# Spacer tiles in SBUF that shift where the weights' halves, the activations and the heads' tiles begin (modulo 256 bytes)

## The chip, the cores and the metric

The kernel runs on one core of one Trainium2 chip. The metric is the device time of one execution in microseconds (us). Three runs of the kernel before took 2298.53, 2303.71 and 2309.76 us, a median of 2303.71 us.

## The reference

One layer of a streaming encoder on a sequence of 256 tokens of 2048 numbers, float32 throughout, conditioned on a vector `c`:

```
mod = silu(c) @ ada_w + ada_b                 # 9 shift/scale/gate vectors
x  += 1/2 * g1 * swiglu(modulate(rms(x)))     # 2048 -> 2 x 5632 -> 2048
h   = modulate(rms(x));  u = h @ w_in         # conv GLU, q, k, v, swish gate, two gates
y_conv = (silu(layer_norm(depthwise_conv31(a * sigmoid(b))))) @ conv_pw_w
y_ret  = (silu(g) * group_norm(retention(rotary(q), rotary(k), v))) @ ret_w_o   # 4 heads
x  += g2 * ((sigmoid(gate_c) * y_conv + sigmoid(gate_r) * y_ret) @ w_out)
x  += 1/2 * g3 * swiglu(modulate(rms(x)))
out = modulate(rms(x)) with its own shift and scale from c
```

Retention works in chunks of 64 tokens; the kernel computes it for a head as a masked 256 x 256 matrix of scores times the values.

## The kernel before, in words

Activations lie transposed: a tile has 128 features in the partitions and 256 tokens along the free dimension. Each weight matrix is read from memory once, in blocks of 128 rows by 128 columns that the host has laid side by side. `raw_load` (L100) brings up to 2048 columns (1 MB) into one of four `raw` buffers on SP's queue. `prep` (L178) then splits each half of it into two tiles of 1024 columns: `hi`, a copy by ScalarE to the type float32r (L189), and `lo`, the remainder `raw - hi`, by VectorE (L192). There are five buffers of each.

Activations are split in the same way, into halves that lie one behind the other: `h` (the modulated input, `new_h`, L259), `s2` (the hidden activations of a feed-forward block, called `s` in the profile, L337), `z` (the conv branch, L485), `r2` and `mg2` (the gated retention output and the merged branches, L595 and L631, called `r` and `mg` in the profile), `q_hi` and so on for the heads (L502).

Each product of two split numbers takes three matmuls: high times high, high times low, low times high. A matmul of TensorE (PE) has a stationary operand of 128 x 128, which a weight load (PEld) brings into the array ahead of it, and an operand that is streamed past it, here 256 columns. In the profile's names `ps<-h,hi` is a matmul that streams `h` past a block of `hi`. Every matmul has a weight load of its own. `gemm` (L206) does most of them: for the blocks of one `hi` tile, two matmuls each with `hi` (L216), then one each with `lo` (L218). `mm3` (L200) does the three in a row (L202, L203, L204). It is used where six PSUM banks are filled side by side from one block row (`across`, L320), in the heads, and in `value` (L523), where the roles are turned: there a slice of `h` is stationary and 512 columns of weights stream past it.

The stages in their order: the first feed-forward block (24 hidden tiles side by side, the rest by `gemm`; its second products stream `s`), the mixer's projections and four heads (`scores` streams q past k, `outputs` streams p past v), the gates and `w_o` (stream `h` and `r2` in turn), the conv branch's gate and `w_pw` (`h` and `z` in turn), `w_out` (streams `mg2`), the second feed-forward block, the final norm. In between, VectorE reduces the 176 tiles of the matrix for `mod` (L110) and applies the conv's taps (L443).

Tiles of a pool are laid out in SBUF in the order in which their tags are first asked for, and pools that are open at the same time lie one behind the other: `keep` (h, x and the constants), then `wp` (raw, a spacer of 64 bytes, hi, lo, a second spacer of 64 bytes), then the pool of the stage. A spacer is a tile that nothing reads; GpSimd (POOL) writes zeros to it once (`apart`, L92). The addresses come out of these sizes alone. A block of weights is 512 bytes of a partition, a half of an activation tile 1024, so all slices of a tile have the same remainder modulo 256. Before the change:

| tile | begins at, modulo 256 | as |
|---|---|---|
| h | 128 | streamed (stationary in `value`) |
| hi, lo | 192 | stationary (streamed in `value`) |
| s, z, r2, mg2 | 0 | streamed |
| q, p | 0 | streamed |
| k, v | 0 | stationary |

## Time and profile before

| | |
|---|---|
| median of three runs | 2303.71 us (2298.53 to 2309.76) |
| the profiled execution's own time | 2299.76 us |
| its span (first to last instruction) | 2298.0 us |
| PE, PEld busy | 98%, 97% |
| VectorE, ScalarE busy | 77%, 46% |
| granted TensorE clock | 0.995 |
| read from memory | 609.77 MB |

Busy time of PE is not PE at its peak: matmuls overlap in the array, a record covers more than the time that a matmul adds, and records in a row leave no gap. What a matmul adds is the distance from its start to the next one's. Where a stretch of the trace holds only matmuls of one kind and PE is never idle in it, that is the stretch's length by the number of matmuls. A stretch counts every record that touches it, so two that began ahead of it (a record of 0.28 us lasts over two distances) are taken off.

### The profile page before, as it was taken

The page shows a single profiled execution, that of the slowest core. Times are in us where ns is not written, and L with a number is a line of the kernel's source. Part 1 is how long each engine was busy: PE and PEld are TensorE (multiplying, and loading weights), DVE is VectorE, ACT ScalarE, POOL GpSimd, SP SyncE. Part 2 cuts the span into 40 slices and gives each one's busy share as a digit, 9 for nine tenths or more (in the row PEclk, how much of TensorE's full clock was granted, in tenths as well). Part 3 has the DMA queues.
Part 4 walks back from the last instruction along what each step waited for, and adds up shares of the span by engine and source line. Part 5 has one row for each costly group of instructions (what it writes and reads, how often), then busy time and mean ns, then how long its engine had stood idle before and what let it go on. Part 6 is the DMA issues. An engine that isn't in the chain of part 4 may idle for free.

```text
span 2298.0 us, 44555 instructions
## 1 busy us (share of the span) xinstructions
PE 2260.2 (98%) x19036; PEld 2234.0 (97%) x19036; DVE 1762.0 (77%) x2212; ACT 1068.4 (46%) x1367; POOL 0.4 (0%) x6
## 2 busy tenths in 40 slices
PE   7999999999999999999999999999999999999997
PEld 6999999999999999999999999999999999999997
DVE  7899887778877679889987787767766666666664
ACT  6544653334444644545544544445544433344443
POOL 0000000000000000000000000000000000000000
PEclk9999999999999999999999999999999999999999
DMA  9989689999888565545776788866777677777662
GB/s 342 357 326 334 222 303 338 328 332 344 335 316 306 173 216 200 170 165 203 266 248 242 261 329 303 332 250 243 288 262 273 243 254 259 269 265 271 248 247 74
DMA packets 92217, 616.86 MB, mean 268 GB/s; under 512 B 10225, under 2 KB 10481, under 8 KB 34673
## 3 DMA queue, kind: packets, MB, share of 16 engines
q1 hardware_dynamic: 90290, 609.81, 73.5%
q10 hardware_dynamic: 1728, 4.20, 0.5%
q8 instruction: 149, 2.44, 0.4%
q14 instruction: 50, 0.41, 0.0%
HBM read 609.77 MB, written 4.19 MB: 267 GB/s over the span
## 4 chain that ended last, share of the span: by engine, by line
PE 97%; DVE 1%; ACT 1%; issue 0%; DVEq 0%; ACTq 0%
PE ps L216 50%; PE ps L218 25%; PE ps L202 7%; PE ps L204 7%; PE ps L203 7%; DVE raw L110 0%; DVE f L668 0%; DVE ssq L272 0%; ACT L245 0%; ACT L238 0%; DVE lo L192 0%; PE gn_v L256 0%; PE gn_m L256 0%; ACT sq L288 0%; PE r L256 0%
## 5 line engine op out<-in xcount | busy, mean ns | idle before, releaser
L189 ACT CAST hi<-raw 128x1024 fp32r<-128x1024 f32 (+2 forms) x864 | 844.7, 986 | 1130.2 <-PE ps L216 639.2
L192 DVE TENSOR_TENSOR lo<-raw,hi 128x1024 fp32r<-128x1024 f32 (+2 forms) x864 | 980.1, 1143 | 452.0 <-ACT hi L189 430.7
L216 PE MATMUL ps<-h,hi 128*128 128x256 f32 x5888 | 731.1, 277 | 0.0
L216 PEld LDWEIGHTS ps<-h,hi 128*128 128x128 f32 x5888 | 698.1, 188 | 0.2
L110 DVE CUSTOM_DVE_ANT_0 raw<-raw,cb,vec 128x2048 f32<-128x2048 f32 x176 | 412.9, 2346 | 3.4 <-DMA raw<-in_adaT 3.4
L218 PE MATMUL ps<-h,lo 128*128 128x256 f32 x2944 | 395.2, 277 | 0.0
L216 PE MATMUL ps<-s,hi 128*128 128x256 f32 x2816 | 362.8, 279 | 0.0
L218 PEld LDWEIGHTS ps<-h,lo 128*128 128x128 f32 x2944 | 362.6, 188 | 0.0
L216 PEld LDWEIGHTS ps<-s,hi 128*128 128x128 f32 x2816 | 345.0, 188 | 0.0
L202 PE MATMUL ps<-h,hi 128*128 128x256 f32 x1152 | 313.8, 280 | 13.9 <-ACT h L305 13.8
L203 PE MATMUL ps<-h,hi 128*128 128x256 f32 x1152 | 318.8, 279 | 3.2 <-DVE h L308 3.2
L204 PE MATMUL ps<-h,lo 128*128 128x256 f32 x1152 | 315.9, 279 | 0.0
L202 PEld LDWEIGHTS ps<-h,hi 128*128 128x128 f32 x1152 | 216.5, 191 | 15.7 <-ACT h L305 15.3
L203 PEld LDWEIGHTS ps<-h,hi 128*128 128x128 f32 x1152 | 219.8, 191 | 3.9 <-DVE h L308 3.7
L204 PEld LDWEIGHTS ps<-h,lo 128*128 128x128 f32 x1152 | 218.1, 191 | 0.0
L218 PE MATMUL ps<-s,lo 128*128 128x256 f32 x1408 | 196.7, 279 | 0.0
L218 PEld LDWEIGHTS ps<-s,lo 128*128 128x128 f32 x1408 | 179.2, 188 | 0.0
L443 DVE SCALAR_TENSOR_TENSOR acc<-y,vec,acc 128x256 f32<-128x256 f32 x240 | 114.3, 481 | 2.7
L216 PE MATMUL ps<-r,hi 128*128 128x256 f32 x512 | 65.8, 280 | 0.0
L216 PE MATMUL ps<-mg,hi 128*128 128x256 f32 x512 | 65.7, 279 | 0.0
L216 PEld LDWEIGHTS ps<-r,hi 128*128 128x128 f32 x512 | 62.6, 188 | 0.0
L216 PEld LDWEIGHTS ps<-mg,hi 128*128 128x128 f32 x512 | 62.6, 188 | 0.0
(149 smaller groups left out, 1181.6 us busy)
## 6 DMA issues: line engine op xcount, KB each, us to landing
raw<-in_adaT SPq DMA_DIRECT2D x176, 1024.0 KB, 5.9
raw<-in_w SPq DMA_DIRECT2D x148, 1024.0 KB, 5.3
raw<-in_w SPq DMA_DIRECT2D x64, 896.0 KB, 5.6
raw<-in_w13s SPq DMA_DIRECT2D x64, 768.0 KB, 6.1
raw<-in_w_v SPq DMA_DIRECT2D x16, 1024.0 KB, 4.9
raw<-in_w_g SPq DMA_DIRECT2D x16, 1024.0 KB, 4.9
raw<-in_w_gr SPq DMA_DIRECT2D x16, 1024.0 KB, 4.9
raw<-in_w_o SPq DMA_DIRECT2D x16, 1024.0 KB, 5.3
```

The costliest lines, as they stand in the source:

```text
L110: tc.keep_in_program_order(V.tensor_tensor_reduce(r, r, cb, 1.0, vec[:, b:b + 1], op0=ALU.mult, op1=ALU.add, accum_out=mod[:, j, t:t + 1]))
L189: A.copy(hi[:, :c1 - c0], r[:, c0:c1])
L192: V.tensor_tensor(lo[:, :c1 - c0], r[:, c0:c1], hi[:, :c1 - c0].bitcast(F32), op=ALU.subtract)
L202: PE.matmul(o, st[0], mv[0], start=start, stop=False, skip_group_check=skip)
L203: PE.matmul(o, st[0], mv[1], start=False, stop=False, skip_group_check=skip)
L204: PE.matmul(o, st[1], mv[0], start=False, stop=stop, skip_group_check=skip)
L216: PE.matmul(o, w[k][0], mv[k][:, half], start=k == 0 and half == 0, stop=False)
L218: PE.matmul(o, w[k][1], mv[k][:, 0], start=False, stop=k == n - 1)
L443: tc.keep_in_program_order(V.scalar_tensor_tensor(out=acc[:, t], in0=y[:, t, k:k + T], scalar=vec[:, dw + k:dw + k + 1], in1=acc[:, t], op ...
```

## The change

It replaces the two spacers of 64 bytes by five of 128, 384, 128, 128 and 320 bytes, three of which lie in the pools of the mixer, and asks for `apart_k` between the tiles of q and k, so that `rotary` for q and for k are two statements:

```diff
-    def apart(i):
-
-        if i not in set_apart:
-            set_apart.add(i)
-            nc.gpsimd.memset(wp.tile([P, 16], F32, name=f"apart{i}", tag=f"apart{i}", bufs=1), 0.0)
+    def apart(pool, name, n):
+
+        if name not in set_apart:
+            set_apart.add(name)
+            nc.gpsimd.memset(pool.tile([P, n // 4], F32, name=name, tag=name, bufs=1), 0.0)
...
-            apart(0)
+            apart(wp, "apart_w", 128)
             hi = wp.tile([P, 1024], F32R, name="hi", tag="hi", bufs=HI)
             A.copy(hi[:, :c1 - c0], r[:, c0:c1])
             lo = wp.tile([P, 1024], F32R, name="lo", tag="lo", bufs=LO)
-            apart(1)
+            apart(wp, "apart_s", 384)
...
+                apart(p1, "apart_p", 128)
                 sc = t512("sc")
                 V.tensor_tensor(sc, two(ps), dm, op=ALU.mult)
                 return halves(sc, "p")
...
-            qk = [rotary(banks[0], "q"), rotary(banks[1], "k")]
+            qk = [rotary(banks[0], "q")]
+            apart(p1, "apart_k", 128)
+            qk.append(rotary(banks[1], "k"))
...
         with tc.tile_pool(name="mix2", bufs=1) as p2:
+            apart(p2, "apart_r", 320)
             r2 = sb(p2, [P, ND, 2, T], "r2", F32R)
```

What it does to the addresses, as the distance from the start of the stationary tile to the start of the streamed one, modulo 256:

| streamed past stationary | before | after |
|---|---|---|
| h past hi, lo | 192 | 128 |
| s past hi, lo | 64 | 128 |
| z past hi, lo | 64 | 128 |
| r2, mg2 past hi, lo | 64 | 192 |
| q past k; p past v | 0 | 128 |
| hi, lo past h (`value`) | 64 | 128 |

Modulo 512 the same distances are 192, 64, 64, 64, 0, 0 and 320 before, and 128 (h), 384 (s, z), 192 (r2, mg2), 384 (q), 128 (p) and 384 (`value`) after.

No instruction of PE, VectorE, ScalarE or SP is added, left out or moved. On GpSimd five memsets stand in the place of two; this is its program after the change, from the first spacer on, with what each waits for (a name in brackets is an engine's or a DMA queue's semaphore):

```order
L96 MEMSET apart_w 128x32
L96 MEMSET apart_s 128x96
L96 MEMSET apart_k 128x32 [waits DVE_49,PE_49]
L96 MEMSET apart_p 128x32
L96 MEMSET apart_r 128x80 [waits DMAHW4_49,DMAHW3_49,DMAHW5_49,DVE_49,DMAHW6_49,PE_49,Pool_49]
```

Four instructions of ScalarE and PE and one DMA of SP now wait for GpSimd too; all but one of them stand far behind the memset that they wait for. The one close by is a cast of ScalarE behind `apart_r`. These are ScalarE's rows after the change where the last head ends and the gates begin; `r_12204` is r2:

```order
L612 ACTIVATE g_12205<-ps 128x512 [waits PE_49]
L565 COPY og<-ps 128x512 [waits PE_49] x2
L189 CAST hi<-raw 128x1024 [waits DVE_49,PE_49]
L604 CAST r_12204<-g_12205 128x2x256 [waits DVE_49,Activation_49,Pool_49]
L189 CAST hi<-raw 128x1024 [waits DMAHW7_49,PE_49]
L457 ACTIVATE gn_mean<-gn_m 128x256 [waits PE_49]
```

The order of these rows is that of before; only the `Pool_49` of the first cast into r2 is new. Behind it in ScalarE's queue stand the casts of the next weights.

## The prediction

> **What bounds the kernel now.** I read the page's busy times and its chain first, then who waits for whom.

> ```profile
> PE 2260.2 (98%) x19036; PEld 2234.0 (97%) x19036; DVE 1762.0 (77%) x2212; ACT 1068.4 (46%) x1367; POOL 0.4 (0%) x6
> PE 97%; DVE 1%; ACT 1%; issue 0%; DVEq 0%; ACTq 0%
> ```

> ```profile
> ACT hi L189 <- PE ps L216: 639.2, 429, 4.4
> DVE lo L192 <- ACT hi L189: 430.7, 406, 3.7
> PE ps L202 <- ACT h L305: 13.8, 3, 5.8
> ```

> PE is the chain that ends last for 97% of the span. ScalarE, which makes the weights' halves, waits 639 us for PE to give a `hi` buffer back, and PE's own longest wait is 13.8 us, at the starts of stages. So the time is the number of matmuls times what each adds, and only a change of that number moves it. The groups of PE, by the tile that is streamed (first name) and loaded (second):

> ```profile
> line engine op names shapes xcount | busy us, mean ns | idle before us <-releasers
> L216 PE MATMUL ps<-h,hi 128*128 128x256 f32 x5888 | 731.1, 277 | 0.0
> L218 PE MATMUL ps<-h,lo 128*128 128x256 f32 x2944 | 395.2, 277 | 0.0
> L216 PE MATMUL ps<-s,hi 128*128 128x256 f32 x2816 | 362.8, 279 | 0.0
> L203 PE MATMUL ps<-h,hi 128*128 128x256 f32 x1152 | 318.8, 279 | 3.2 <-DVE h L308 3.2
> L204 PE MATMUL ps<-h,lo 128*128 128x256 f32 x1152 | 315.9, 279 | 0.0
> L202 PE MATMUL ps<-h,hi 128*128 128x256 f32 x1152 | 313.8, 280 | 13.9 <-ACT h L305 13.8
> L218 PE MATMUL ps<-s,lo 128*128 128x256 f32 x1408 | 196.7, 279 | 0.0
> L216 PE MATMUL ps<-r,hi 128*128 128x256 f32 x512 | 65.8, 280 | 0.0
> L216 PE MATMUL ps<-mg,hi 128*128 128x256 f32 x512 | 65.7, 279 | 0.0
> L202 PE MATMUL ps<-hi,h 128*128 128x512 f32 x128 | 50.6, 395 | 0.0
> L218 PE MATMUL ps<-mg,lo 128*128 128x256 f32 x256 | 35.4, 279 | 0.0
> L218 PE MATMUL ps<-r,lo 128*128 128x256 f32 x256 | 35.3, 279 | 0.0
> L216 PE MATMUL ps<-z,hi 128*128 128x256 f32 x256 | 32.8, 280 | 0.0
> L218 PE MATMUL ps<-z,lo 128*128 128x256 f32 x128 | 17.7, 279 | 0.0
> L203 PE MATMUL ps<-p_lo,v_hi 128*128 128x256 f32 x32 | 9.1, 283 | 0.0
> L204 PE MATMUL ps<-q_hi,k_lo 128*128 128x256 f32 x16 | 4.5, 283 | 0.0
> ```

> That is 12,288 matmuls with h, 4,224 with s, 384 with z, 1,536 with r and mg; p, q and `value` have three such groups each, 96, 48 and 384. All but `value` have the same shape. What each adds is read from stretches that hold one kind. The columns are the stretch, its length, then for each engine its busy time and instructions, the granted clock, the DMA's share and GB/s:

> ```profile
> 340.00:480.00 140.00, 140.00 (x1191) 140.00 (x1190) 111.68 (x130) 50.70 (x56) 0.00 (x0) 1.00 0.91 329
> 500.00:640.00 140.00, 140.00 (x1238) 140.00 (x1237) 111.45 (x118) 62.15 (x79) 0.00 (x0) 1.00 0.89 332
> 836.00:845.00 9.00, 9.00 (x41) 7.38 (x40) 9.00 (x18) 3.67 (x4) 0.00 (x0) 1.00 0.48 160
> 1048.00:1058.00 10.00, 10.00 (x90) 10.00 (x90) 9.77 (x15) 5.66 (x9) 0.00 (x0) 1.00 0.50 192
> 1059.00:1061.40 2.40, 2.40 (x22) 2.40 (x22) 2.40 (x5) 2.37 (x4) 0.00 (x0) 1.00 0.85 345
> 1068.00:1079.00 11.00, 11.00 (x96) 11.00 (x95) 9.59 (x12) 6.11 (x9) 0.00 (x0) 1.00 0.50 179
> 1345.00:1440.00 95.00, 95.00 (x809) 95.00 (x808) 75.33 (x77) 41.77 (x45) 0.00 (x0) 1.00 0.85 311
> 1455.00:1545.00 90.00, 90.00 (x767) 90.00 (x766) 66.02 (x74) 36.82 (x40) 0.00 (x0) 1.00 0.80 296
> ```

> PE is busy through each, at the full clock. With two records taken off for those begun earlier, s adds 140/1189 = 117.7 ns a matmul, h 140/1236 = 113.3, mg 90/765 = 117.6, p past v 2.4/20 = 120, and a 512-column matmul of `value` 9/39.3 = 229. Same engine, clock, shape and loop (s, h and mg all come from `gemm`), and neither VectorE nor DMA differs between the first two rows: what does is where the tiles lie. The distance from loaded to streamed is 192 for h, 64 for s, mg and `value`, and 0 for p. So a distance has a price here: 0 gives 120, 64 gives 117.7, 192 gives 113.3. But it is not all. The stretches 1068 to 1079 (11/94 = 117.0) and 1345 to 1440 (95/807 = 117.7) hold h at 192 too, alone and with z, and h there costs what s does. How many there are:

> ```profile
> L216 PE MATMUL ps<-h,hi 128*128 128x256 f32 x671 | 85.9, 281 | 0.0
> L218 PE MATMUL ps<-h,lo 128*128 128x256 f32 x336 | 46.4, 281 | 0.0
> ```

> ```profile
> L216 PE MATMUL ps<-h,hi 128*128 128x256 f32 x64 | 8.4, 284 | 0.0
> L218 PE MATMUL ps<-h,lo 128*128 128x256 f32 x31 | 4.3, 281 | 0.0
> ```

> The first pair is 1257.5 to 1452 us, the second 1068 to 1079: together 1,102 slow matmuls with h. Both stretches begin right behind the four plain float32 matmuls of a norm's sums; h has two regimes at one distance, and an interruption can move it from one to the other.

> **The change, part by part.** All prices but one are in the trace. r2 and mg2 go from 64 to 192: 1,536 times (117.7 - 113.3 = 4.4 ns) = 6.8 us less. Everything else goes to 128, which no matmul of before has. Its neighbours are 64 (117.7) and 192 (113.3), its opposite is 0 (120). From above I bound it by the nearer slow neighbour, 117.7. From below, a curve that is even around the circle (a mean plus a cosine) through the three prices has its mean at (117.7 + 113.3)/2 = 115.5 and gives 115.5 - (120 - 115.5) = 111.0 at 128. I take 113.3: the better neighbour, and the lowest value that any long stretch shows; h keeps to it in `gemm` and in `mm3` alike, which looks like a floor rather than a point on a curve, and the point farthest from the worst should be on it.

> By that value, s gives 4,224 x 4.4 = 18.6 us, z 384 x 4.4 = 1.7, the slow h 1,102 x 4.4 = 4.8, the other h nothing, p and q 144 x 6.7 = 1.0, and `value` 384 x (229 - 2 x 113.3 = 2.4) = 0.9. With r2 and mg2 the sum is 33.8 us.

> [...]

> What rides along is cheap. The memsets:

> ```profile
> L96 POOL MEMSET apart<- 128x16 f32 x2 | 0.2, 112 | 0.3 <-POOLq L756 0.3
> ```

> Three more at about 0.1 us, up to six times as wide, stay below 1 us each. Only the last has somebody near behind it, the first cast into r2, with casts of weights behind that. r2 itself is not streamed until all gates of that loop are done, and the `hi` casts have 639 us of waiting for PE to spend, five buffers ahead; if that cover were gone, the price would be one memset, under 1 us. VectorE's and ScalarE's operands move too; a few per cent on either would vanish in their 23% and 54% of idle time. Would a faster s stage starve? It would need 329 x 117.7/113.3 = 342 GB/s and a DMA share of 0.945; VectorE would be at 83%.

> ```profile
> GB/s 342 357 326 334 222 303 338 328 332 344 335 316 306 173 216 200 170 165 203 266 248 242 261 329 303 332 250 243 288 262 273 243 254 259 269 265 271 248 247 74
> ```

> The second slice moved 357, so it just fits. If it were held at 329, the first block's s (half of 18.6 us) would give nothing, 9.3 us back.

> **Rivals.** *Lower still.* At 128 the streams may clear each other entirely and 113.3 may itself hold a price. For it: three distances, three prices, and the curve through them leads to 111.0. Against: nothing in the trace stays below 113. All that goes to 128 is 12,288 + 4,224 + 384 + 144 = 17,040 matmuls; 2.3 ns less each is 39 us more, 73 us in all: 2227. [...]

> *Slower.* 128 may be like 64. Then h, which is two thirds of PE's time, leaves the best distance in the trace for the sake of tiles a third as many. The 11,186 fast matmuls with h would lose 4.4 ns each, 49.2 us; s, z and the slow h would gain nothing; r2 and mg2 would still give 6.8 and p and q 0.3: 42 us slower, 2342. Against the forecast it decides from a price of 113.3 + 33.8/17,040 us = 115.3 ns at 128. At 120, as for distance 0, it would be 80 us. For it: 113.3 is a regime that h can fall out of, and 192 may be special because of who comes first at a place, not because it is far. Against: 64 and 192 are equally far from 128, so a dependence by nearness favours the better half.

> *Nothing.* The price may hang on the regime that a run of matmuls enters, not on the distance (the 1,102 slow ones at 192 speak for it), or on addresses modulo 512, where s would be at 384 and h at 128, both unseen. If s, h, z stay as they are and only r2 and mg2 follow, 2293; if nothing follows, 2299.8. [...]

> **How the numbers follow.** The sum is made against the profiled execution's own 2299.8 us, of which 2298.0 are the span: 2299.8 - 33.8 = 2266. The median of the three runs is 3.9 us higher, and they lie 11 us apart; so 0.5%, 11.5 us, is about what a measurement of this kernel can tell from no change. Chances: the forecast, with slow stretches of h or DMA waits left over, 0.47; lower still 0.22; nothing or r2 and mg2 alone 0.12; slower 0.19. The range takes in the first three and their edges: from 2215, somewhat beyond 111.0 ns, to 2306, nothing at the median; most of the slower case stays outside. Faster by over 0.5%: 0.47 + 0.22 and a few mixed cases, 0.72. Within 0.5%: 0.10. Slower: 0.18.

> **What would show it.** The stretch of s (about 330 to 480 us) should hold a matmul every 113.3 ns, that is 1,238 records in 140 us rather than 1,191; h in 500 to 640 should stay at 1,238; mg should rise from 767 in 90 us to about 796; p past v should go from 0.12 us to 0.113. PE must stay busy through each, and ScalarE's wait for PE should shrink by some 30 us with no wait of PE for `hi` in its place. h with fewer than 1,215 records in 140 us (115.3 ns) proves the forecast wrong and the slower rival right; more than 1,250 proves the lower one. A shift in VectorE's or ScalarE's durations would not matter unless PE begins to wait.

## The result, and the profile after

The change makes the kernel slower: 2362.86 us (median of four runs, 2358.31 to 2367.42) against 2306.59 us (2298.53 to 2309.76), a ratio of 1.0249 with a 95% interval of 1.021 to 1.0289. Ratios that stand with an interval leave out any run over 1.5% above the fastest of its kernel. The forecast was 2266. Busy times and chain of the changed kernel:

```profile
PE 2318.5 (98%) x19036; PEld 2291.3 (97%) x19036; DVE 1765.6 (75%) x2212; ACT 1070.2 (45%) x1367; POOL 0.8 (0%) x9
PE 97%; DVE 1%; ACT 1%; issue 0%; DVEq 0%
```

PE bounds it as before, with the same number of matmuls. VectorE and ScalarE do the same work in the same time, 3.6 and 1.8 us more. PE's busy time grew by 58.3 us, the span by 58.5. So each matmul adds more. The stretches by stage (length, then busy time and count for PE, PEld, VectorE, ScalarE and GpSimd, then clock, DMA share and GB/s), in this order s, h, `value`, h behind a norm's sums, mg, h of the second block:

```profile
360.00:500.00 140.00, 140.00 (x1182) 140.00 (x1182) 112.59 (x131) 52.68 (x57) 0.00 (x0) 1.00 0.92 336
530.00:670.00 140.00, 140.00 (x1182) 140.00 (x1181) 107.53 (x112) 59.61 (x75) 0.00 (x0) 1.00 0.86 316
860.00:869.00 9.00, 9.00 (x40) 7.33 (x39) 9.00 (x19) 4.76 (x8) 0.00 (x0) 1.00 0.67 229
1115.00:1185.00 70.00, 70.00 (x586) 70.00 (x584) 65.66 (x91) 34.30 (x41) 0.00 (x0) 1.00 0.71 252
1500.00:1570.00 70.00, 70.00 (x620) 70.00 (x620) 54.63 (x60) 30.56 (x33) 0.00 (x0) 1.00 0.85 316
1600.00:1840.00 240.00, 240.00 (x2025) 240.00 (x2024) 160.66 (x197) 109.21 (x147) 0.00 (x0) 1.00 0.75 265
```

With two records taken off as before, h adds 140/1180 = 118.6 ns a matmul where it added 113.3. Its 1,182 records in 140 us are below the 1,215 named ahead as the sign of the slower rival. The s stretch has the same 118.6 (117.7 before). mg, the one tile here that went to 192, adds 70/618 = 113.3 (117.6 before). 128 has a second price as well: in the fourth stretch, h adds 70/584 = 119.9. That holds for 670 matmuls, behind the sums of a norm. h and s now have the same distance and the same price, although one is at 128 and the other at 384 modulo 512. h's own address did not change at all; only the weights that are loaded beside it moved.

The sum closes to about 1 us: 11,186 x 5.3 ns for h that was fast = 59.3 us, 1,102 x 0.9 for h that was slow = 1.0, 4,608 x 0.9 for s and z = 4.1, less 1,536 x 4.4 for r and mg = 6.8, makes 57.6. The 670 at the second price add 0.9. `value` rose too, from 229 to 9/38.3 = 235 in the stretches shown; over all its matmuls the distance from start to start rose from 229 to 232, which is 1.2 us for 384. That makes 59.7; measured were 58.5.

The new memsets on GpSimd cost nothing. The rows are the last of them, and ScalarE's longest wait:

```profile
L96 POOL MEMSET apart_r<- 128x80 f32 x1 | 0.2, 165 | 283.6 <-PE ps L204 283.6
ACT hi L189 <- PE ps L216: 684.9, 447, 2.1
```

`apart_r` takes 165 ns and starts at 1095.18 us. The first cast into r2, which waits for it, starts at 1097.95, right behind a cast of weights and with no idle time of ScalarE before it. ScalarE's wait for PE grew from 639 to 685 us: with a slower PE, ScalarE has more time to spare.

### The profile page after: what moved, and what is told of

Same layout as the page of the kernel before. It is cut to its first block, busy times and chain, and to the rows that moved or that the text cites. A ratio compares the mean times of both kernels' runs of the same rounds, so it can differ in the third digit from the quotient of the medians.

```text
span 2356.5 us, 44565 instructions
## 1 busy us (share of the span) xinstructions
PE 2318.5 (98%) x19036; PEld 2291.3 (97%) x19036; DVE 1765.6 (75%) x2212; ACT 1070.2 (45%) x1367; POOL 0.8 (0%) x9
## 4 chain that ended last, share of the span: by engine, by line
PE 97%; DVE 1%; ACT 1%; issue 0%; DVEq 0%
PE ps L216 50%; PE ps L218 25%; PE ps L202 7%; PE ps L203 7%; PE ps L204 7%; DVE f L672 0%; DVE raw L110 0%; DVE ssq L272 0%; ACT L245 0%; ACT L238 0%; DVE lo L192 0%; PE gn_v L256 0%; PE gn_m L256 0%; ACT sq L288 0%; PE r L256 0%
## 5 line engine op out<-in xcount | busy, mean ns | idle before, releaser
L189 ACT CAST hi<-raw 128x1024 fp32r<-128x1024 f32 (+2 forms) x864 | 846.2, 985 | 1189.1 <-PE ps L216 684.9
L192 DVE TENSOR_TENSOR lo<-raw,hi 128x1024 fp32r<-128x1024 f32 (+2 forms) x864 | 981.7, 1143 | 508.3 <-ACT hi L189 492.3
L216 PE MATMUL ps<-h,hi 128*128 128x256 f32 x5888 | 759.7, 282 | 0.0
L216 PEld LDWEIGHTS ps<-h,hi 128*128 128x128 f32 x5888 | 725.1, 188 | 0.2
L218 PE MATMUL ps<-h,lo 128*128 128x256 f32 x2944 | 409.7, 282 | 0.0
L218 PEld LDWEIGHTS ps<-h,lo 128*128 128x128 f32 x2944 | 375.2, 188 | 0.0
L216 PE MATMUL ps<-s,hi 128*128 128x256 f32 x2816 | 365.4, 281 | 0.0
L216 PEld LDWEIGHTS ps<-s,hi 128*128 128x128 f32 x2816 | 347.5, 188 | 0.0
L202 PE MATMUL ps<-h,hi 128*128 128x256 f32 x1152 | 319.4, 285 | 13.8 <-ACT h L305 13.8
L203 PE MATMUL ps<-h,hi 128*128 128x256 f32 x1152 | 324.7, 284 | 3.4 <-DVE h L308 3.4
L204 PE MATMUL ps<-h,lo 128*128 128x256 f32 x1152 | 321.7, 284 | 0.0
L202 PEld LDWEIGHTS ps<-h,hi 128*128 128x128 f32 x1152 | 216.7, 191 | 15.5 <-ACT h L305 15.3
L203 PEld LDWEIGHTS ps<-h,hi 128*128 128x128 f32 x1152 | 219.8, 191 | 4.1 <-DVE h L308 3.9
L204 PEld LDWEIGHTS ps<-h,lo 128*128 128x128 f32 x1152 | 218.3, 191 | 0.0
L218 PE MATMUL ps<-s,lo 128*128 128x256 f32 x1408 | 198.3, 281 | 0.0
L218 PEld LDWEIGHTS ps<-s,lo 128*128 128x128 f32 x1408 | 180.4, 188 | 0.0
L216 PE MATMUL ps<-r,hi 128*128 128x256 f32 x512 | 63.7, 277 | 0.0
L216 PE MATMUL ps<-mg,hi 128*128 128x256 f32 x512 | 63.4, 276 | 0.0
L216 PEld LDWEIGHTS ps<-r,hi 128*128 128x128 f32 x512 | 60.7, 188 | 0.0
L216 PEld LDWEIGHTS ps<-mg,hi 128*128 128x128 f32 x512 | 60.5, 188 | 0.0
```

The lines of the kernel that those rows point to most:

```text
L189: A.copy(hi[:, :c1 - c0], r[:, c0:c1])
L192: V.tensor_tensor(lo[:, :c1 - c0], r[:, c0:c1], hi[:, :c1 - c0].bitcast(F32), op=ALU.subtract)
L202: PE.matmul(o, st[0], mv[0], start=start, stop=False, skip_group_check=skip)
L203: PE.matmul(o, st[0], mv[1], start=False, stop=False, skip_group_check=skip)
L204: PE.matmul(o, st[1], mv[0], start=False, stop=stop, skip_group_check=skip)
L216: PE.matmul(o, w[k][0], mv[k][:, half], start=k == 0 and half == 0, stop=False)
```

## The experiments

Edits are against the changed kernel unless said otherwise; numbers in the code are bytes.

**h alone back to 192 (h_back).** A spacer ahead of `h`, and the next one shorter, so that the weights stay where the change put them:

```diff
+    nc.gpsimd.memset(keep.tile([P, 16], F32, name="apart_h", tag="apart_h", bufs=1), 0.0)
     crow = sb(keep, [1, D], "crow", tag="h")
...
-            apart(wp, "apart_w", 128)
+            apart(wp, "apart_w", 64)
```

> The changed kernel with h alone moved by 64 bytes (and what lies between h and the weights with it), so that h is 192 past hi and lo again, at another address than before; hi and lo stay where the change put them. Theory (distance): h falls from 118.7 to 113.4 ns, 12,288 x 5.3 = 65 us, to about 2298 to 2303 us, ratio to before 0.997 to 0.999; s stays at 118.7. Rival (where the weights' halves lie by themselves is what made h slow): h stays at 118.7, about 2363 us, ratio 1.025.

Measured: 2309.12 us (2305.85 to 2318.65, 10 runs), 1.0011 times the kernel before (0.9983 to 1.0039). Its stretches of h, s, and h again:

```profile
100.00:320.00 220.00, 220.00 (x1871) 220.00 (x1870) 194.41 (x272) 113.52 (x173) 0.00 (x0) 1.00 0.80 285
360.00:500.00 140.00, 140.00 (x1182) 140.00 (x1181) 112.22 (x131) 51.47 (x56) 0.00 (x0) 1.00 0.92 335
520.00:670.00 150.00, 150.00 (x1326) 150.00 (x1325) 119.34 (x127) 65.53 (x83) 0.00 (x0) 1.00 0.88 331
```

h is at 150/1324 = 113.3 again in 520 to 670, at an address that it never had, past weights that lie at 0 and not at 192; s stays at 118.6. So nearly all of the loss was h's distance of 128, and neither tile's place by itself. In this profile the first stretch of h, at the same 192, is in the slow regime (220/1869 = 117.7), and so is the one from 2020 to 2201 us (160/1359 = 117.7 from 2030 to 2190). That is why the time is some 7 us above the 2298 to 2303 expected.

**Everything at 192 (all192).**

```diff
-            apart(wp, "apart_w", 128)
+            apart(wp, "apart_w", 64)
...
-            apart(wp, "apart_s", 384)
+            apart(wp, "apart_s", 192)
...
-                apart(p1, "apart_p", 128)
+                apart(p1, "apart_p", 192)
...
-            apart(p1, "apart_k", 128)
+            apart(p1, "apart_k", 64)
...
-            apart(p2, "apart_r", 320)
```

> Every streamed tile 192 bytes past the weights it streams by (h, s, z, r2, mg2, q, p); value stays at 64. Theory (the distance from loaded to streamed, modulo 256, sets the price): 113.4 ns a matmul in the stretches of s, z, r and mg as for h, so some 33 us below the kernel before, ratio about 0.986; about 0.988 if h keeps its slow stretches. Rival (the price belongs to the tile or to the regime its stage falls into, and r2 and mg2 were lucky): s and z stay near 117.7, ratio 0.997 or above.

Measured: 2286.09 us, 0.9891 times the kernel before (0.9856 to 0.9925): faster than both kernels, by less than hoped, and the ten runs lie between 2267.57 and 2301.84. By the medians of all runs it is 2286.09/2302.93 = 0.993. Two stretches of h, one of s, then h again, s and h of the second block:

```profile
95.00:220.00 125.00, 125.00 (x1105) 125.00 (x1105) 115.32 (x147) 58.67 (x82) 0.00 (x0) 1.00 0.91 327
235.00:335.00 100.00, 100.00 (x851) 100.00 (x851) 84.16 (x129) 56.20 (x92) 0.00 (x0) 1.00 0.71 248
360.00:490.00 130.00, 130.00 (x1106) 130.00 (x1105) 101.90 (x121) 46.33 (x52) 0.00 (x0) 1.00 0.91 326
520.00:670.00 150.00, 150.00 (x1276) 150.00 (x1275) 116.73 (x122) 64.00 (x82) 0.00 (x0) 1.00 0.86 318
1880.00:2000.00 120.00, 120.00 (x1061) 120.00 (x1060) 79.16 (x90) 47.44 (x51) 0.00 (x0) 1.00 0.77 276
2030.00:2170.00 140.00, 140.00 (x1238) 140.00 (x1237) 91.12 (x96) 61.89 (x78) 0.00 (x0) 1.00 0.73 261
```

h starts at 125/1103 = 113.3, and in the second block s is at 120/1059 = 113.3 and h at 140/1236 = 113.3. From 227 until 845 us, though, h and s alike are at 117.7 to 117.8 (100/849, 130/1104, 150/1274). These are about 5,160 matmuls, each 4.4 ns dearer, 23 us in all; at the fast price, this execution of 2290.87 us would have taken 2268. So the distance sets which prices are to be had, 113.3 and 117.8 at 192, and the regime which of them is paid, whatever the tile. The moment of the change can be seen in the order of time (rows of PE, and the cast; rows of other engines between them are left out):

```profile
226.26 0.41 ACT L311 CAST h<-xr 128x256 fp32r<-128x256 f32 x1
226.28 0.28 PE L202 MATMUL ps<-h,hi 128*128 128x256 f32 x1
226.39 0.28 PE L203 MATMUL ps<-h,hi 128*128 128x256 f32 x1
226.50 0.28 PE L204 MATMUL ps<-h,lo 128*128 128x256 f32 x1
226.72 0.74 PE L202 MATMUL ps<-h,hi 128*128 128x256 f32 x4
```

Starts are 0.11 us apart until 226.50, and the next is 0.22 later: it starts 0.05 us behind the end of ScalarE's cast of the last piece of h, at 226.67. The four matmuls of the last row take 0.46 us from the first start to the last (0.74 less a record of 0.28), 0.11 more than three distances of 117.8 ns, so one of them is late too. From 235 us on the stretch above has them 117.8 ns apart.

**The same kernel again (all192_b)**, on the chip of the two kernels that follow it here.

> The kernel of all192 again, on the chip and in the rounds of the kick. Theory (two regimes, entered by chance): again a scatter of some 30 us, between 2267 (no slow stretch) and 2300; median 2275 to 2290. Rival (the scatter of all192 was that chip's): under 10 us of scatter.

Measured: 2288.83 us, six runs from 2269.32 to 2325.97, 0.9881 times the kernel before (0.983 to 0.9932), and 0.994 by the medians of all runs. The slowest run lies 26 us above the scatter that was expected. The profile is of an execution of 2271.13 us; its stretches of s, h and s again:

```profile
350.00:480.00 130.00, 130.00 (x1150) 130.00 (x1149) 102.81 (x121) 46.42 (x52) 0.00 (x0) 1.00 0.92 332
520.00:650.00 130.00, 130.00 (x1150) 130.00 (x1149) 107.08 (x112) 59.31 (x76) 0.00 (x0) 1.00 0.92 345
675.00:750.00 75.00, 75.00 (x639) 75.00 (x638) 56.30 (x62) 31.56 (x35) 0.00 (x0) 1.00 0.82 302
```

The s and h that were slow in the other profile are at 130/1148 = 113.2 here; only the third stretch is slow, at 75/637 = 117.7. That regime lasts from 668 to 753 us, 718 matmuls or 3 us more; at the fast price this execution, too, would have taken 2268 us. The forecast's price for s at 192 holds where the regime is fast, and DMA keeps up with it, at 332 GB/s in the stretch of s and 345 in that of h. The same program thus has stretches that are fast in one execution and slow in another, and the difference between the two profiled times is theirs.

**Other distances (sweep_a and sweep_b).** Two kernels with one distance to a tile, exchanged between them; this is the first:

```diff
-            apart(wp, "apart_w", 128)
+            apart(wp, "apart_w", 32)
...
-            apart(wp, "apart_s", 384)
+            apart(wp, "apart_s", 160)
...
+        apart(pool, "apart_z", 192)
         y = sb(pool, [P, NC, PAD + T + 2], "y")
...
-            apart(p2, "apart_r", 320)
+            apart(p2, "apart_r", 192)
```

Its `apart_p` and `apart_k` are 96. In the second kernel the four are 96, 224, 64 and 64, and the last two 224.

> Other distances, one to a tile: h 224, s 160, z 96, r2 and mg2 32, q 160, p 96. Theory (distance): one price per stretch, and the same for the same distance in the other sweep, whatever the tile; between known neighbours, about 117 for h (224), 116 for s (160), 118 for z (96), 119 for r and mg (32); about 2340 us. Rival (tile or regime): the same distance costs different tiles prices over 1 ns apart.

> The distances of the other sweep, exchanged: h 160, s 224, z 32, r2 and mg2 96, q 32, p 224. Theory (distance): h at what s had at 160, s at what h had at 224, z at what r had at 32, r and mg at what z had at 96, each within 0.5 ns; about 2330 us by neighbours. Rival (tile or regime): they keep the prices of their tiles.

Measured: 2355.83 and 2362.12 us, one execution each, 16 and 32 us above what was expected. The first kernel's stretches of h (224), s (160), s later (160) and mg (32):

```profile
100.00:320.00 220.00, 220.00 (x1862) 220.00 (x1861) 193.65 (x270) 111.99 (x171) 0.00 (x0) 1.00 0.80 282
360.00:500.00 140.00, 140.00 (x1196) 140.00 (x1195) 112.81 (x131) 51.28 (x57) 0.00 (x0) 1.00 0.94 338
700.00:770.00 70.00, 70.00 (x592) 70.00 (x592) 54.06 (x60) 29.63 (x32) 0.00 (x0) 1.00 0.85 312
1500.00:1570.00 70.00, 70.00 (x602) 70.00 (x601) 53.88 (x60) 29.72 (x32) 0.00 (x0) 1.00 0.82 307
```

And the second's, h (160), s (224), h later (160), mg (96), and z (32), for which only the matmuls with z are counted:

```profile
100.00:320.00 220.00, 220.00 (x1857) 220.00 (x1856) 193.44 (x269) 112.27 (x171) 0.00 (x0) 1.00 0.80 282
360.00:500.00 140.00, 140.00 (x1185) 140.00 (x1185) 110.50 (x129) 50.66 (x56) 0.00 (x0) 1.00 0.92 332
520.00:670.00 150.00, 150.00 (x1281) 150.00 (x1280) 117.51 (x124) 64.31 (x83) 0.00 (x0) 1.00 0.87 323
1500.00:1570.00 70.00, 70.00 (x586) 70.00 (x585) 53.54 (x59) 29.01 (x31) 0.00 (x0) 1.00 0.81 299
1385.00:1391.30 6.30, 5.82 (x48) 5.72 (x48) 0.00 (x0) 0.00 (x0) 1.00 0.72 241
```

224 costs h 220/1860 = 118.3 and s 140/1183 = 118.3. 160 has two regimes as well, and both tiles show both: s 117.3 and 70/590 = 118.6, h 118.6 and 150/1279 = 117.3. 32 costs mg 70/600 = 116.7, 96 costs it 70/584 = 119.9, and z at 96 in the first kernel costs 120.0. So the price follows the distance and not the tile, with one exception: z at 32 costs (5.82 - 0.28)/47 = 117.9 in each of its eight stretches, 1.2 ns more than mg, where at most 0.5 was expected. It may be a second price of 32. Or it counts that the two are 256 bytes apart modulo 512 (288 for z, 32 for mg). No run separates these. Of the values between, 160, 224 and 96 were guessed too low, and 32 too high.

**Half steps, and 512 (sweep_c).** The kernel with everything at 192, s 256 bytes further on, and h and r2 begun 16 bytes into longer tiles (mg2 in the same way):

```diff
-            apart(wp, "apart_s", 192)
+            apart(wp, "apart_s", 448)
...
-        return sb(keep, [P, ND, 2, T], "h", F32R)
+        full = sb(keep, [P, ND * 2 * T + 8], "h", F32R)
+        return full[:, 4:4 + ND * 2 * T].rearrange("p (n u t) -> p n u t", n=ND, u=2)
```

> Half steps beside 192: h at 176, r2 and mg2 at 208, by views that begin 16 bytes into their tiles; s and z at 192 modulo 256 but 448 modulo 512. Theory (distance modulo 256, with a notch at 192): s and z at 113.3 or 117.8; h and r between 113.3 and the prices of 160 and 224 (117.3 to 118.7). If the notch is as narrow as a line of 32 bytes, h and r are near 117 or above, about 2320 us; if 16 bytes don't matter, all is at 113.3, about 2270. Rival (512 counts): s and z above 118.

Measured: 2352.14 us, one execution. h (176), s (192), s of the second block, mg (208):

```profile
100.00:320.00 220.00, 220.00 (x1847) 220.00 (x1846) 192.27 (x268) 112.17 (x172) 0.00 (x0) 1.00 0.80 281
360.00:500.00 140.00, 140.00 (x1191) 140.00 (x1190) 108.57 (x129) 50.17 (x56) 0.00 (x0) 1.00 0.91 328
1920.00:2050.00 130.00, 130.00 (x1149) 130.00 (x1149) 87.45 (x97) 51.30 (x55) 0.00 (x0) 1.00 0.77 273
1500.00:1570.00 70.00, 70.00 (x590) 70.00 (x589) 53.38 (x60) 28.68 (x31) 0.00 (x0) 1.00 0.81 302
```

16 bytes to either side of 192 the gain is gone: h 220/1845 = 119.2, mg 70/588 = 119.0. s, at 192 modulo 256 but 448 modulo 512, has the two prices of 192, 117.7 and 130/1147 = 113.3. So at 192, as at 128 (h at 128 and s at 384 in the changed kernel, both at 118.6), 256 bytes more changed nothing, and 192 is a notch narrower than 16 bytes to a side. The time is 32 us above the 2320 expected because h was put at 117 and cost 119.2. Three more kernels (half_a, half_b and quarter) looked for others, with the weights' halves begun 16 or 8 bytes into wider tiles, four `lo` buffers instead of five, and spacers to suit:

```diff
-RAW, HI, LO = 4, 5, 5
+RAW, HI, LO = 4, 5, 4
...
-            hi = wp.tile([P, 1024], F32R, name="hi", tag="hi", bufs=HI)
+            hi = wp.tile([P, 1088], F32R, name="hi", tag="hi", bufs=HI)[:, 4:]
```

> The weights' halves begin 16 bytes into their tiles (four lo buffers instead of five make the room), so distances fall between the steps so far: h 16, s 48, z 80, r2 and mg2 112, q and p 64. Theory (192 is a notch and everything else lies at 116.5 to 120 ns): no stretch below 116, h and s about 118 to 119; about 2360 us. Rival (more notches lie between the steps): a stretch at 113.3 or below.

> As half_a with h 144, s 240, z 48, r2 and mg2 80. Theory (one notch): no stretch below 116 ns; z as s at 48 in half_a, r as z at 80 there, within 0.7 ns; about 2360 us. Rival (more notches): a stretch at 113.3 or below.

> As half_a with the halves 8 bytes into their tiles: h 184, s 248, z 56, r2 and mg2 120. Theory (the notch at 192 is narrower than 16 bytes): h at 184 tells whether 8 bytes are still within it; above 117 if it is a matter of 16-byte pieces, 113.3 if it is a slope. Everything else above 116; about 2360 us, or 2310 with h in the notch.

Measured: 2356.27, 2378.04 and 2354.46 us, one execution each. In the first, h (16), s (48), mg (112), h of the second block (16):

```profile
100.00:235.00 135.00, 135.00 (x1128) 135.00 (x1127) 118.88 (x149) 57.09 (x78) 0.00 (x0) 1.00 0.86 312
360.00:480.00 120.00, 120.00 (x1031) 120.00 (x1030) 93.50 (x110) 41.21 (x46) 0.00 (x0) 1.00 0.91 322
1500.00:1585.00 85.00, 85.00 (x710) 85.00 (x710) 62.21 (x71) 33.70 (x37) 0.00 (x0) 1.00 0.81 300
1600.00:1900.00 300.00, 300.00 (x2559) 300.00 (x2558) 203.20 (x248) 140.82 (x189) 0.00 (x0) 1.00 0.73 259
```

In the second, whose granted clock was 0.95 throughout, h (144), s (240), mg (80), and z (48) with its own matmuls alone:

```profile
100.00:250.00 150.00, 150.00 (x1252) 150.00 (x1251) 133.89 (x175) 70.11 (x101) 0.00 (x0) 0.95 0.86 307
360.00:500.00 140.00, 140.00 (x1186) 140.00 (x1185) 110.24 (x128) 49.21 (x56) 0.00 (x0) 0.95 0.91 327
1510.00:1580.00 70.00, 70.00 (x595) 70.00 (x594) 54.46 (x62) 29.28 (x32) 0.00 (x0) 0.95 0.86 322
1379.50:1386.00 6.50, 5.76 (x48) 5.68 (x48) 0.00 (x0) 0.00 (x0) 0.95 0.93 349
```

In the third, h (184) and s of the second block (248):

```profile
100.00:230.00 130.00, 130.00 (x1101) 130.00 (x1100) 115.85 (x147) 55.23 (x77) 0.00 (x0) 1.00 0.87 314
1925.00:2060.00 135.00, 135.00 (x1170) 135.00 (x1169) 87.93 (x97) 52.65 (x56) 0.00 (x0) 1.00 0.77 268
```

16 costs 135/1126 = 119.9 in the first block and 300/2557 = 117.3 in the second, so it has two prices too. 48 costs 120/1029 = 116.6, 112 85/708 = 120.1, 144 120.0, 240 118.2, 80 118.0, 184 130/1099 = 118.3, 248 135/1168 = 115.6; mg at 120, in the third kernel, 118.0 (595 records in 70 us). So the prices run from 115.6 to 120.1 without a slope that leads anywhere, but for one notch at 192, 8 bytes below which the price is already 118.3. Across tiles the prices agree here: z at 48 costs (5.76 - 0.28)/47 = 116.6 in the second kernel, as s does in the first. The theory's "no stretch below 116" missed 248 by 0.4 ns; nothing but 192 comes to 113.3.

**What changes the regime (kick and jolt).** The kernel with everything at 192, with two overwritten matmuls at distance 0 put in at 24 places (in `pair`, ahead of `across` in the first block as below, and at the start of `side_by_side`):

```diff
+    pairs_done = [0]
+    def kick(o, w):
+        for _ in range(2):
+            PE.matmul(o, w[0][2][:, 0:P], w[0][2][:, 0:T], start=True, stop=True)
...
-            gemm(ps[:, u * T:(u + 1) * T], ws[u](), mv)
+            w = ws[u]()
+            if u == 0 and pairs_done[0] % 12 == 0:
+                kick(ps[:, 0:T], w)
+            pairs_done[0] += u
+            gemm(ps[:, u * T:(u + 1) * T], w, mv)
...
+            if begins and i % 2 == 0:
+                kick(banks[0][:, 0:T], w)
```

> All at 192 as in all192, and two extra matmuls whose result is overwritten, 24 times over the kernel (at every other start of six banks and at every twelfth pair): both operands from one hi tile, so distance 0. They add 48 x 0.12 = 5.8 us of work. Theory (at 192 there are two regimes, 113.3 and 117.8 ns; an interruption throws a stretch into the slow one and it stays there; distance 0 leads back, as p did in the kernel before each time): slow stretches end at the next kick, so 2267 + 6 + a few, some 2275 us, with less scatter than all192. Rival (regimes are not reset by what runs before): all192 plus 6 us, about 2290, with the same scatter.

Measured: 2310.49 us, twelve runs from 2304.99 to 2313.99, 1.0013 times the kernel before (0.9988 to 1.0037). Stretches on either side of the kicks at 632, 1648 and 1784 us:

```profile
510.00:630.00 120.00, 120.00 (x1061) 120.00 (x1060) 95.02 (x103) 53.83 (x68) 0.00 (x0) 1.00 0.89 336
640.00:675.00 35.00, 35.00 (x299) 35.00 (x298) 26.52 (x27) 14.91 (x19) 0.00 (x0) 1.00 0.85 315
1570.00:1640.00 70.00, 70.00 (x621) 70.00 (x620) 55.26 (x80) 40.61 (x62) 0.00 (x0) 1.00 0.86 295
1655.00:1780.00 125.00, 125.00 (x1064) 125.00 (x1063) 79.69 (x91) 52.59 (x66) 0.00 (x0) 1.00 0.71 255
1790.00:1940.00 150.00, 150.00 (x1326) 150.00 (x1325) 98.05 (x111) 62.57 (x75) 0.00 (x0) 1.00 0.74 261
```

The first is at 120/1059 = 113.3, the second at 35/297 = 117.8, then 113.1, 117.7 and 113.3 (one record more or less is 0.2 ns in 70 us). Each kick turns the regime over, also out of the fast one; in the whole trace this holds for all 20 kicks with a long stretch on either side. My theory that distance 0 leads back to it falls; so does the rival, since what runs before does set the regime. The scatter shrank to 9 us, which fits much the same stretches being slow in every run, but only one of the twelve was profiled. The same places with plain float32 matmuls:

```diff
-            PE.matmul(o, w[0][2][:, 0:P], w[0][2][:, 0:T], start=True, stop=True)
+            PE.matmul(o, ones, cb[:, 0:T], start=True, stop=True)
```

> The places of the kick, but with two plain float32 matmuls of constants (as in a norm's sums) in place of the matmuls at distance 0; their result is overwritten. About 24 x 0.98 = 23 us of work more. Theory (such an interruption changes the regime at 192 by chance): of the stretches between them a good part at 117.8, changing at the jolts and not in between; about 2267 + 23 + 15 to 45 us. Rival (regimes come from the stage): the same stages fast and slow as in all192.

Measured: 2320.8 us, one execution, within the 2305 to 2335 expected. Stretches on either side of the jolts at 635, 1657 and 1788 us:

```profile
640.00:675.00 35.00, 35.00 (x299) 35.00 (x299) 27.50 (x29) 14.82 (x19) 0.00 (x0) 1.00 0.85 314
1570.00:1650.00 80.00, 80.00 (x682) 80.00 (x680) 62.63 (x89) 45.80 (x72) 0.00 (x0) 1.00 0.80 280
1665.00:1780.00 115.00, 115.00 (x1018) 115.00 (x1017) 76.46 (x87) 51.01 (x64) 0.00 (x0) 1.00 0.72 259
1795.00:1955.00 160.00, 160.00 (x1361) 160.00 (x1360) 100.11 (x113) 64.09 (x76) 0.00 (x0) 1.00 0.71 249
```

117.8, 80/680 = 117.6, 115/1016 = 113.2 and 160/1359 = 117.7: these turn it over too, and not by chance as I had expected, but again at all 20 places with a long stretch on either side. Waits can do it as well: between two jolts, the regime also changed at 234 us, behind two starts 0.18 us apart. But not every break does. In all192 the stretch stayed fast over two starts 0.97 us apart at 91 us (113.4 ns a matmul from 60 to 220 us without that gap) and over the sums of a norm at 1081. In the kernel before, h fell out of the fast regime behind such sums at 1067 (117.0 from 1068 to 1079, as in the prediction's rows). At 128 it is the same: in the changed kernel h stayed at 118.7 over the sums at 1100 (10.8/91 from 1080.9 to 1091.7, and 118.7 from start to start behind them) and was at 119.9 behind those at 1113.

## Why the prediction was wrong, point by point

- *PE bounds the kernel, and only the price of a matmul moves it*: right. The span grew by 58.5 us, PE's busy time by 58.3.
- *The price goes with the distance from loaded to streamed*: right, and now shown for 192: the same distance at other addresses has the same prices (h in h_back, s in all192: 113.3 and 117.7), and so has 448 (s in sweep_c: 113.3 and 117.7). It isn't the whole of it, since several distances have two prices, and z at 32 differs from mg at 32.
- *r2 and mg2 to 192, 6.8 us less*: right, 113.3 ns as forecast.
- *128 taken at 113.3, "the point farthest from the worst should be on it"*: this is the step that failed. 128 costs 118.6, in places 119.9. I had treated the price as a smooth function around the circle and read three points as a trend. The prices read later show one notch at 192; 16 bytes to either side of it a matmul costs 119.2 and 119.0. Both bounds failed with it: 118.6 lies above the upper one, the slower neighbour's 117.7, and the cosine's 111.0 has no counterpart: the lowest price read is 113.1, at 192.
- *The slower rival*: right in kind, that h leaves the best distance in the trace and two thirds of PE's time with it, and right that 192 isn't good for being far from 0. The reason that it gave, who comes first at a place, no run tests. Its 42 us were 58.5 because 128 is 0.9 ns worse than 64. Its chance of 0.19 rested on the argument "64 and 192 are equally far from 128", which carries no weight for something that isn't smooth.
- *Two regimes at one distance*: seen in the trace of before, but used only as 4.8 us of the sum. all192 shows its weight: it makes the difference between 2268 us and the 2290.87 of one profiled execution. The reading that an interruption can move h between regimes was right.
- *Memsets, casts behind them, VectorE's and ScalarE's operands, DMA*: nothing, as said (`apart_r` 165 ns with no idle time of ScalarE behind it, VectorE and ScalarE 3.6 and 1.8 us busier in a span 58.5 us longer, PE busy through every stretch shown).

What stays open: every matmul of these runs has a weight load of its own, so whether the prices need one was not shown. Why 192 and not 64, why a distance has two prices, and how to hold the fast regime, were not found either.

## What to carry to other kernels

A price that has been measured at three settings is known at three settings: before moving the largest user of a known good one to an unmeasured one, measure that one, or move the others to the good one. Here the latter, everything at 192, gave 0.989 of the time before (0.9856 to 0.9925; 0.993 by the medians of all runs), and the price of 113.3 could be read off the trace of before. Where a kernel is nothing but matmuls, take their start-to-start distance by stage, and look at the operands' relative addresses when equal shapes differ.
